# A seventh seven-product unit in the second half of the FFNs' second product

## The chip, the cores and the metric

The kernel runs on one core of a Trainium2 chip. The metric is the device time of one execution in microseconds. Every run is timed alone; the number shown is the median of several runs.

## The reference

One decoder layer on a sequence of 256 tokens with a model width of 2048, in float32: a gated FFN half-step, a mixer of two linear-attention branches, and a second gated FFN half-step. Each of them has a norm on its input and a norm on its output before the residual add. The change touches the FFNs alone:

```
def swiglu(x, w_gate, w_up, w_down):
    return (jax.nn.silu(x @ w_gate) * (x @ w_up)) @ w_down

f1 = swiglu(rms_norm(h, ffn1_pre_norm), ffn1_w_gate, ffn1_w_up, ffn1_w_down)
h = h + 0.5 * rms_norm(f1, ffn1_post_norm)
```

The hidden width is 5504. So the second product of an FFN, the one with w_down, is 256 x 5504 by 5504 x 2048.

## The kernel before

**Products in three parts.** Each float32 operand is split in two: hi, a copy rounded to the type that TensorE multiplies (ScalarE, L153), and lo, the rest (VectorE, L155). A product of two operands is then three matmuls: hi by hi, lo by hi, and hi by lo (L159, L160, L161). One matmul takes a 128 x 128 piece of the activations and 512 columns of weights.

**Units and sevens.** The 256 tokens are two blocks of rows (t = 0, 1). The contraction is cut into k-tiles of 128; two of them are a unit. For one unit and 1024 columns of weights (two blocks of 512) the plain way has eight products: two k-tiles, two blocks of rows, two blocks of columns. The other way is that of Strassen and Winograd: seven products of sums of blocks, and some additions. Here it is the method `seven` of the class `Blocks`. It loads four blocks of weights (four loads of 256 KB on SP's queue), makes the sums of weights on VectorE (all of them through `add`, L245, so the trace shows them under that line: `wsum`, `raw`, `wsum`), splits them on ScalarE (L280 to L286) and VectorE (`wlo`, `wsuml`), and issues 21 matmuls. Four of the seven products gather in accumulators of their own (`p1`, `p5`, `p6`, `p7`), which `share` and `close` add to the four outputs at the end. A plain unit loads its weights in two pieces of 512 KB and issues 24 matmuls.

A seven needs four sums of the activations too (`four_sums`: d, s2, s3, s4, L205 to L208), split into hi and lo. They depend on the unit alone and not on the columns of the weights.

**The second product.** `down_proj` runs over the output in two halves of 1024 columns (`hf`). Each half goes through the 43 k-tiles in order. A list of units says which go by seven products; before a unit on the list is reached, `sums_of` makes its sums, unless they are kept from the first half. Before the change the first half had the units 3, 7, 9, 11, 15 and 19, the second 3, 5, 7, 11, 13 and 15. The sums of 3, 7, 11 and 15 were kept for both halves: three sets in tiles that had held the FFN's input (`xhi0`, `xlo0`, `xhi1`, half of each used) and the fourth in two of the three `tmp` tiles. The sums of the other units lay in the ring of four tiles (`hkhi`, `hklo`) that also takes the split activations of each unit.

The last seven k-tiles of the second half (36 to 42, `DTAIL`) have their weights split ahead into tiles that have become free (`held`), so that the products of the first block of rows can end before those of the second begin, and its norm can start. The first of these tiles is in `xhi1`. The weights pass through rings of five tiles each: `raw` (as loaded), `whi`, `wlo`. The sums of weights of a seven lie in three `row` tiles, of which there are three.

**What sets the order.** Each engine works through its own list of instructions in order. The list is set at build time by a planner, which may move an instruction ahead of others that wait; the program gives the dependences and a rank. At the end of the second half of the first FFN the loads and splits of the mixer's first weights (`following`, `w_in`) are issued between the last products.

Of the kernel before, what the change touches and what calls it, by code (L numbers as in the profile page):

```python
# [7 lines left out]
F32 = mybir.dt.float32  # L8
F32R = mybir.dt.float32r
# [7 lines left out]
P = 128  # L17
# [7 lines left out]
CB = 512  # L25
# [7 lines left out]
AHEAD = 3  # L33
SUMS = (2, 4, 6)
FOUR = (2, 4, 5, 6)
DSUMS = (3, 7, 11, 15)
DMORE = ((9, 19), (5, 13))
DTAIL = 7
O_GQ, O_GK, O_GV, O_GO, O_CODE = 0, 512, 1024, 2048, 3072
O_HQ, O_HF, O_HI, O_HO, O_ZG, O_ZH = 3088, 4112, 5136, 6160, 7184, 9232  # L40
# [48 lines left out]
def kernel(ctx: ExitStack, tc: tile.TileContext, a: dict, out: bass.AP):  # L89
# [9 lines left out]
    work = ctx.enter_context(tc.tile_pool(name="work", bufs=2))  # L99
# [5 lines left out]
    def nm(s):  # L105
        uid[0] += 1
        return f"{s}_{uid[0]}"
# [102 lines left out]
    def operand_sums(x, new_part, out, more=True):  # L210

        yield
        for units in [SUMS] + [(u,) for u in FOUR if more and u not in SUMS]:
            if units[0] in out:
                continue
            n = len(units)
            us = slice(units[0], units[-1] + 1, units[1] - units[0] if n > 1 else 1)
            ab = row_tile("sums").rearrange("p i c -> p (i c)")[:, :4 * n * P].rearrange(  # L220
                "p (t u k) -> p t u k", t=NT, u=n)
            for t in range(NT):
                hi, lo = [part[t].bitcast(F32).rearrange("p (u i) c -> p u (i c)", i=2)[:, us, :]
                          for part in x[:2]]
                nc.vector.tensor_tensor(ab[:, t], hi, lo, op=ALU.add)
                yield
            s = row_tile("sums").rearrange("p i c -> p (i c)")[:, :4 * n * P].rearrange(
                "p (m u c) -> p m u c", m=4, u=n)
            four_sums(*[ab[:, t, :, i * P:(i + 1) * P] for t in range(NT) for i in range(2)],
                      *[s[:, m] for m in range(4)])  # L230
            for j, u in enumerate(units):
                yield
                hi, lo = new_part(0), new_part(1)
                split_into(hi, lo, s[:, :, j, :])
                out[u] = hi, lo
# [145 lines left out]
    def row_tile(s, dt=F32):  # L381
        return rows.tile([P, 3, CB], dt, tag="row", name=nm(s))
# [20 lines left out]
    def tiles4(x):  # L403
        return x.rearrange("p (k c) -> p k c", c=P)
# [12 lines left out]
    def joined(dst, turned):  # L417

        nc.scalar.activation(dst.bitcast(U16).rearrange("p j (k h) -> p h j k", h=2),
                             turned.rearrange("p (h j) k -> p h j k", h=2), AF.Copy)  # L420
# [11 lines left out]
    def lhs_of(x):  # L432
        def lhs(t, kt):

            side.until(lambda: x[2][t] > kt)
            return x[0][t][:, kt, :], x[1][t][:, kt, :]
        return lhs
# [167 lines left out]
    def down_proj(w_dram, nkt, lhs, sums_of, post, pre, wpost, ys, homes, following):  # L605
# [30 lines left out]
        for hf in range(2):  # L636
# [4 lines left out]
            n = nkt - DTAIL if hf else nkt  # L641
            units = sorted(DSUMS + DMORE[hf])
            kt = 0
# [49 lines left out]
    def ffn(pre, x, rs, post, pre_next, begin=None, ready=(), then=None):  # L693
        with ExitStack() as fctx:
            fwork = fctx.enter_context(tc.tile_pool(name=nm("fwork"), bufs=2, reuse_waits="tile"))
            fpool = fctx.enter_context(tc.tile_pool(name=nm("fpool"), bufs=1, reuse_waits="tile"))
            sums = {}

            def new_part(i):
                s = ("hkhi", "hklo")[i]  # L700
                return fwork.tile([P, 2, NT * P], F32R, tag=s, name=nm(s), bufs=4)

            def x_sums():
                return operand_sums(
                    x, lambda i: tiles4(new_part(i).rearrange("p i c -> p (i c)")), sums)

            raws = begin(x_sums) if begin else ()

            def held(w):
                hi, lo = [fpool.tile([P, 2, w], F32R, tag="hT", name=nm("held"), bufs=11)  # L710
                          for _ in range(2)]
                return [(hi, lo)]

            xl = lhs_of(x)
            hT = {}

            blocks = [FIRST] + list(range(0, FIRST, CB))

            def finish(t, f0, w, u, s):
                n = w // P  # L720
                nc.vector.scalar_tensor_tensor(s[:, :w], u[:, :w], rs[t], s[:, :w],
                                               op0=ALU.mult, op1=ALU.mult)
                yield
                turned = turn(s[:, :w], fwork.tile([P, CB], F32, tag="halves", name=nm("halves")))
                for _ in range(6):
                    yield
                joined(hT[f0 // CB][:, :n, t * P:(t + 1) * P], turned)

            for j, f0 in enumerate(blocks):
                w = min(CB, DFF - f0)  # L730
                following = [first_of(a[pre + s], f1) for f1 in blocks[j + 1:j + 2]
                             for s in ("_w_gate", "_w_up")]
                if j or begin:
                    g, u, ready = gemm_pair(
                        [(a[pre + "_w_gate"], f0), (a[pre + "_w_up"], f0)], w, xl, sums, ready,
                        following, () if j else raws, (FOUR if j % 2 else SUMS) if j else ())
                else:
                    g = gemm_block(a[pre + "_w_gate"], f0, w, xl, held=held, ready=ready)
                    ready = ()
                s = []  # L740
                for t in range(NT):
                    st = fwork.tile([P, CB], F32, tag="silu", name=nm("silu"))
                    nc.scalar.activation(st[:, :w], g[t][:, :w], AF.Silu, scale=rs[t])
                    s.append(st)
                if not (j or begin):
                    side.spawn(x_sums())
                    u = gemm_block(a[pre + "_w_up"], f0, w, xl)
                hT[f0 // CB] = fpool.tile([P, 4, NT * P], F32, tag="hT", name=nm("hT"), bufs=11)
                for t in range(NT):
                    side.spawn(finish(t, f0, w, u[t], s[t]))  # L750
            def lhs():
                parts = {}

                def get(t, kt):
                    g2 = kt // 2
                    if g2 not in parts:
                        n = min(2, FKT - g2 * 2)
                        hi, lo = new_part(0), new_part(1)
                        c = g2 % 2 * 2
                        split_into(hi[:, :n, :], lo[:, :n, :], hT[g2 // 2][:, c:c + n, :])  # L760
                        parts[g2] = hi, lo
                    hi, lo = parts[g2]
                    return hi[:, kt % 2, t * P:(t + 1) * P], lo[:, kt % 2, t * P:(t + 1) * P]
                return get


            def in_x(s, dt):
                return tpool.tile([P, 4, CB], dt, tag=s, name=nm("held"))

            wpost = in_x("xlo1", F32)  # L770
            def sums_of(u):
                v = hT[u // 2][:, u % 2 * 2:u % 2 * 2 + 2, :]
                f = row_tile("sums")[:, 0, :]
                four_sums(v[:, 0, :P], v[:, 1, :P], v[:, 0, P:], v[:, 1, P:],
                          *[f[:, k * P:(k + 1) * P] for k in range(4)])
                if any(u in more for more in DMORE):
                    hi, lo = [new_part(i).rearrange("p i c -> p (i c)") for i in range(2)]
                elif u != DSUMS[-1]:
                    home = in_x(("xhi0", "xlo0", "xhi1")[DSUMS.index(u)], F32R)
                    hi, lo = home[:, 0, :], home[:, 1, :]  # L780
                else:
                    hi, lo = [work.tile([P, CB], F32R, tag="tmp", name=nm("sums"), bufs=3)
                              for _ in range(2)]
                split_into(hi, lo, f)
                return tiles4(hi), tiles4(lo)

            def held_x(w):
                v = in_x("xhi1", F32R)
                return [(v[:, 0:2, :], v[:, 2:4, :])]

            ytags = ["halves", "halves", "silu", "silu"]

            def ys():
                return fwork.tile([P, CB], F32, tag=ytags.pop(), name=nm("y"))

            return down_proj(a[pre + "_w_down"], FKT, lhs, sums_of, post, pre_next,
                             [wpost[:, n, :] for n in range(4)], ys,
                             [held_x] + [ring_alloc] * 2 + [held] * 4, then)
# [588 lines left out]
```

## Time and profile before

| | us |
|---|---|
| median of 3 runs | 2067.72 (2065.52 to 2069.54) |
| the profiled execution, its own time | 2064.64 |
| its span, first to last instruction | 2062.7 |
| TensorE busy (matmuls) | 2046.9 |
| VectorE busy | 1857.5 |
| ScalarE busy | 1321.9 |
| first FFN, second product | about 455 to 678 |
| last FFN, second product | about 1816 to 2054 |

The page gives each engine's busy time as a union of its instructions, in which matmuls overlap each other; it says where TensorE waits and not how fast it works. In a group of instructions the first number behind the bar is the busy time, then the mean length of one in ns, and behind the second bar the idle time of the engine just before these instructions and what ended it. In a row of the timeline the first two numbers are the start and the length in us. In a row of stretches each engine has its busy time with the count of its instructions in brackets.

### The profile page before, as it was taken

How to read it: one execution, taken by the hardware profiler on the slowest of the kernel's cores; microseconds unless marked ns; L12 is line 12 of the kernel's file. 1: busy time of each engine (PE TensorE's matmuls, PEld its weight loads, DVE VectorE, ACT ScalarE, POOL GpSimd, SP SyncE). 2: the span in 40 equal slices, each digit the busy share in tenths (PEclk: the TensorE clock that was granted, in tenths of full speed). 3: DMA queues.
4: the chain of work that ended last, by engine and by line, in shares of the span. 5: the costliest groups of instructions: out<-in, count | busy, mean ns of one | idle time of the engine just before them, and what ended most of it. 6: DMA issues, size and time to landing. Idle time of an engine off the chain costs nothing. (4 is left out here: it accounts for less than half of the span.)

```text
span 2062.7 us, 28952 instructions
## 1 busy us (share of the span) xinstructions
PE 2046.9 (99%) x10305; PEld 1700.0 (82%) x10305; DVE 1857.5 (90%) x2187; ACT 1321.9 (64%) x1730; POOL 41.1 (2%) x87
## 2 busy tenths in 40 slices
PE   9999999999999999999999999999999999999998
PEld 9888888888888888878888887788888888888886
DVE  7999999998999789989999896678999999989996
ACT  7666666666666576577655556665666666766663
POOL 1000000000000100000000000010000000000000
PEclk9999999999999999999999999999999999999999
DMA  8767677776767467556565668846767767776663
GB/s 261 217 207 240 194 222 219 210 229 208 232 194 233 143 200 225 155 181 187 173 202 183 186 220 212 258 158 202 230 195 217 228 210 220 222 239 191 212 210 129
DMA packets 254553, 425.60 MB, mean 206 GB/s; under 512 B 71924, under 2 KB 80311, under 8 KB 254408
## 3 DMA queue, kind: packets, MB, share of 16 engines
q1 hardware_dynamic: 194896, 401.80, 61.7%
q10 hardware_dynamic: 59512, 21.94, 5.4%
q8 instruction: 81, 1.33, 0.3%
q14 instruction: 64, 0.52, 0.1%
HBM read 406.11 MB, written 4.19 MB: 199 GB/s over the span
## 5 line engine op out<-in xcount | busy, mean ns | idle before, releaser
L155 DVE TENSOR_TENSOR wlo<-raw,whi 128x1024 fp32r<-128x1024 f32 (+3 forms) x498 | 582.9, 1185 | 69.0 <-ACT whi L153 66.9
L153 ACT ACTIVATE whi<-raw 128x1024 fp32r<-128x1024 f32 (+3 forms) x498 | 504.2, 1025 | 193.7 <-PE c L160 67.1
L159 PE MATMUL c<-whi,xhi 128*128 128x512 f32 (+1 forms) x1270 | 494.6, 390 | 0.0
L160 PE MATMUL c<-whi,xlo 128*128 128x512 f32 (+1 forms) x1270 | 491.3, 387 | 0.0
L161 PE MATMUL c<-wlo,xhi 128*128 128x512 f32 (+1 forms) x1270 | 491.3, 387 | 0.0
L245 DVE TENSOR_TENSOR wlo<-raw,whi 128x1024 fp32r<-128x1024 f32 x252 | 299.6, 1219 | 35.2 <-ACT whi L284 22.3
L161 PEld LDWEIGHTS c<-wlo,xhi 128*128 128x128 f32 x1270 | 238.4, 188 | 47.5
L159 PEld LDWEIGHTS c<-whi,xhi 128*128 128x128 f32 x1270 | 238.4, 188 | 47.0 <-ACT xhi L487 0.6
L160 PEld LDWEIGHTS c<-whi,xlo 128*128 128x128 f32 x1270 | 238.5, 188 | 46.3
L284 ACT ACTIVATE whi<-raw 128x1024 fp32r<-128x1024 f32 x126 | 133.1, 1056 | 199.7 <-DVE raw L245 98.3
L245 DVE TENSOR_TENSOR wsuml<-wsum,wsumh 128x1536 fp32r<-128x1536 f32 x126 | 220.8, 1752 | 8.4 <-ACT wsumh L286 8.4
L161 PE MATMUL c<-wlo,hkhi 128*128 128x512 f32 x558 | 217.2, 389 | 0.0
L159 PE MATMUL c<-whi,hkhi 128*128 128x512 f32 x558 | 217.2, 389 | 0.0
L160 PE MATMUL c<-whi,hklo 128*128 128x512 f32 x558 | 217.1, 389 | 0.0
L282 ACT ACTIVATE wsumh<-wsum 128x1024 fp32r<-128x1024 f32 x126 | 132.6, 1052 | 89.6 <-DVE wsum L245 65.7
L280 ACT ACTIVATE whi<-raw 128x1024 fp32r<-128x1024 f32 x126 | 132.4, 1051 | 62.7 <-PE c L160 49.6
L245 DVE TENSOR_TENSOR wsum<-raw,raw 128x1024 f32<-128x1024 f32 x126 | 153.7, 1219 | 15.7 <-DMA raw<-in_ffn_w_down_dram 13.8
L159 PEld LDWEIGHTS c<-whi,hkhi 128*128 128x128 f32 x558 | 104.8, 188 | 21.8
L161 PEld LDWEIGHTS c<-wlo,hkhi 128*128 128x128 f32 x558 | 104.8, 188 | 21.8 <-DVE wlo L245 0.3
L160 PEld LDWEIGHTS c<-whi,hklo 128*128 128x128 f32 x558 | 104.8, 188 | 21.7
L245 DVE TENSOR_TENSOR c<-c,psum 128x512 f32<-128x512 f32 x135 | 87.4, 693 | 10.4 <-PE c L161 10.1
L245 DVE TENSOR_TENSOR wsum<-raw 128x512 f32<-128x512 f32 x126 | 87.0, 691 | 3.6
(346 smaller groups left out, 3166.3 us busy)
## 6 DMA issues: line engine op xcount, KB each, us to landing
raw<-in_ffn_w_down_dram SPq DMA_DIRECT2D x124, 512.0 KB, 4.7
raw<-in_w_in_dram SPq DMA_DIRECT2D x104, 512.0 KB, 4.5
raw<-in_ffn_w_gate_dram SPq DMA_DIRECT2D x90, 512.0 KB, 4.7
raw<-in_ffn_w_up_dram SPq DMA_DIRECT2D x90, 512.0 KB, 4.3
raw<-in_ffn_w_gate_dram SPq DMA_DIRECT2D x140, 256.0 KB, 3.9
raw<-in_ffn_w_up_dram SPq DMA_DIRECT2D x140, 256.0 KB, 3.6
raw<-in_w_in_dram SPq DMA_DIRECT2D x128, 256.0 KB, 3.6
raw<-in_ffn_w_down_dram SPq DMA_DIRECT2D x96, 256.0 KB, 3.8
```

The costliest lines, as they stand in the source:

```text
L153: last[0] = nc.scalar.activation(hi, src, AF.Copy)
L155: nc.vector.tensor_tensor(lo, src, hi.bitcast(F32), op=ALU.subtract)
L159: nc.tensor.matmul(ps, lhsT=xhi, rhs=whi, start=start, stop=False)
L160: nc.tensor.matmul(ps, lhsT=xlo, rhs=whi, start=False, stop=False)
L161: nc.tensor.matmul(ps, lhsT=xhi, rhs=wlo, start=False, stop=stop)
L245: return nc.vector.tensor_tensor(o, x, y, op=op)
L280: nc.scalar.activation(ahi, ra, AF.Copy)
L282: nc.scalar.activation(hi[:, 0:2, :], wsum[:, 0:2, :], AF.Copy)
L284: nc.scalar.activation(bhi, rb, AF.Copy)
```

## The change

Unit 9 joins the units whose sums are kept, so the list of the second half becomes 3, 5, 7, 9, 11, 13, 15; that of the first half stays as it is. In the second half the k-tiles 18 and 19 thus go through `seven` in place of `plain`. The five kept sets of sums lie in pairs in the three input tiles: 3 and 7 in `xhi0`, 9 and 11 in `xlo0`, 15 in `xhi1`. No set lies in a `tmp` tile any more, and that of unit 9 no longer takes a place in the ring.

```
-DSUMS = (3, 7, 11, 15)
-DMORE = ((9, 19), (5, 13))
+DSUMS = (3, 7, 9, 11, 15)
+DMORE = ((19,), (5, 13))
...
-            wpost = in_x("xlo1", F32)
+            wpost, homes = in_x("xlo1", F32), []
...
-                if any(u in more for more in DMORE):
+                if u in DSUMS:
+                    i = DSUMS.index(u)
+                    if i % 2 == 0:
+                        homes.append(in_x(("xhi0", "xlo0", "xhi1")[i // 2], F32R))
+                    hi, lo = [homes[-1][:, 2 * (i % 2) + k, :] for k in range(2)]
+                else:
                     hi, lo = [new_part(i).rearrange("p i c -> p (i c)") for i in range(2)]
-                elif u != DSUMS[-1]:
-                    home = in_x(("xhi0", "xlo0", "xhi1")[DSUMS.index(u)], F32R)
-                    hi, lo = home[:, 0, :], home[:, 1, :]
-                else:
-                    hi, lo = [work.tile([P, CB], F32R, tag="tmp", name=nm("sums"), bufs=3)
-                              for _ in range(2)]
                 split_into(hi, lo, f)
```

## The prediction

> **What bounds the kernel now.** I read the page first, then busy time by stretches (the first half of the second product in the first FFN, the mixer, four stretches of that FFN's second half: units 3 to 6, 7 to 10, 11 to 15, and what follows), then what TensorE waited for.
>
> ```profile
> span 2062.7 us, 28952 instructions
> PE 2046.9 (99%) x10305; PEld 1700.0 (82%) x10305; DVE 1857.5 (90%) x2187; ACT 1321.9 (64%) x1730; POOL 41.1 (2%) x87
> ...
> PEclk9999999999999999999999999999999999999999
> ```
> ```profile
> core 0: us, PE busy (x) PEld busy (x) DVE busy (x) ACT busy (x) POOL busy (x), PEclk, DMA share, GB/s
> 455.00:567.00 112.00, 112.00 (x494) 92.26 (x493) 100.71 (x127) 71.48 (x88) 0.00 (x0) 1.00 0.71 221
> 678.00:1500.00 822.00, 816.58 (x4836) 677.59 (x4835) 716.12 (x940) 518.29 (x773) 28.77 (x57) 1.00 0.64 195
> ...
> 585.60:606.00 20.40, 20.40 (x92) 16.90 (x91) 19.58 (x23) 14.62 (x19) 0.00 (x0) 1.00 0.56 176
> 606.00:627.00 21.00, 21.00 (x95) 17.38 (x94) 18.85 (x24) 12.17 (x14) 0.00 (x0) 1.00 0.74 234
> 627.00:652.20 25.20, 25.20 (x113) 20.88 (x112) 24.11 (x25) 18.23 (x23) 0.00 (x0) 1.00 0.68 212
> 652.20:678.00 25.80, 25.01 (x110) 20.22 (x109) 19.32 (x23) 11.37 (x16) 1.20 (x4) 1.00 0.71 239
> ```
> ```profile
> PE acc L159 <- ACT whi L153: 2.7, 1, 2.7
> ...
> PE c L160 <- DVE hklo L155: 0.8, 1, 0.8
> PE p L161 <- DVE wsuml L245: 0.6, 1, 0.6
> ```
>
> TensorE never pauses in the sevens of these halves, at a full granted clock. It starts a matmul every 112.00 / 494 = 0.227 us; a row's 0.39 us is the length of one matmul in a pipe, not its price. But VectorE is close behind: 24.11 of 25.20 us (96%) while units 11 to 15 run. And the second half of the first FFN ends with a wait of TensorE (0.8 us as idle time, 1.1 by starts, below) on VectorE's hklo.
>
> **The change, part by part.** In both FFNs, k-unit 9 (two k-tiles) of the second half goes from plain to seven products. The sums of its left operand were made in the first half already, so no sums are added there.
>
> *TensorE.* A plain unit is 2 k-tiles x 4 products x 3 = 24 matmuls, a seven 7 x 3 = 21. Three go per FFN: 3 x 0.227 = 0.68 us, 1.36 us in all. They go out of an engine without pauses, so this is the most that TensorE alone can give.
>
> The Trainium skill, page "TensorE: Matmul & The Clock Gate", section "Wait — 56ns, not 53.3ns?", gives N / 2.4 GHz + 2.5 ns between starts, 215.7 ns at 512 columns. An estimate by that page would be 6 x 0.2157 = 1.29 us; the trace's 0.227 decides.
>
> *VectorE and ScalarE.* The two splits of weights (whi on ScalarE, wlo on VectorE) stay. What a seven has beyond a plain unit:
>
> ```profile
> L245 DVE TENSOR_TENSOR wsuml<-wsum,wsumh 128x1536 fp32r<-128x1536 f32 x126 | 220.8, 1752 | 8.4 <-ACT wsumh L286 8.4
> L245 DVE TENSOR_TENSOR wsum<-raw,raw 128x1024 f32<-128x1024 f32 x126 | 153.7, 1219 | 15.7 <-DMA raw<-in_ffn_w_down_dram 13.8 <-DMA raw<-in_w_in_dram 1.2 <-DMA raw<-in_ffn_w_up_dram 0.4
> L282 ACT ACTIVATE wsumh<-wsum 128x1024 fp32r<-128x1024 f32 x126 | 132.6, 1052 | 89.6 <-DVE wsum L245 65.7 <-PE c L160 18.5 <-DVE raw L245 3.9
> L245 DVE TENSOR_TENSOR wsum<-raw 128x512 f32<-128x512 f32 x126 | 87.0, 691 | 3.6
> L245 DVE TENSOR_TENSOR raw<-wsum,raw 128x512 f32<-128x512 f32 x126 | 86.8, 689 | 2.8
> L286 ACT ACTIVATE wsumh<-wsum 128x512 fp32r<-128x512 f32 x126 | 77.7, 617 | 5.5 <-DVE wsum L245 5.5
> ```
>
> VectorE: 1.752 + 1.219 + 0.691 + 0.689 = 4.35 us. Its instructions overlap by 0.08 us (below: wsuml from 644.65 for 1.75, the next from 646.32), so four of them take 4.03 us of its time. ScalarE: 1.052 + 0.617 = 1.67 us, hidden, for it is idle 7 us in 25.
>
> *Is there room on VectorE?* The lead is the time from the end of wsuml to the first matmul that reads it. Rows of VectorE and TensorE: first half of the first FFN, unit 11; its second half, units 7 and 15.
>
> ```profile
> 515.50 1.75 DVE L245 TENSOR_TENSOR wsuml<-wsum,wsumh 128x1536 fp32r<-128x1536 f32 x1
> ...
> 516.92 0.39 PE L160 MATMUL p<-wsumh,held 128*128 128x512 f32 x1
> 517.31 0.50 PE L161 MATMUL p<-wsuml,held 128*128 128x512 f32 x1
> 517.64 0.39 PE L159 MATMUL p<-wsumh,held 128*128 128x512 f32 x1
> ...
> 604.30 1.75 DVE L245 TENSOR_TENSOR wsuml<-wsum,wsumh 128x1536 fp32r<-128x1536 f32 x1
> 609.25 0.39 PE L161 MATMUL p<-wsuml,held 128*128 128x512 f32 x1
> ...
> 644.65 1.75 DVE L245 TENSOR_TENSOR wsuml<-wsum,wsumh 128x1536 fp32r<-128x1536 f32 x1
> 646.32 0.69 DVE L155 TENSOR_TENSOR hklo<-hT,hkhi 128x512 fp32r<-128x512 f32 x1
> 650.72 0.39 PE L161 MATMUL p<-wsuml,sums 128*128 128x512 f32 x1
> ```
>
> At unit 7 the lead is 609.25 - 606.05 = 3.2 us, at unit 15 it is 650.72 - 646.40 = 4.3. The added seven takes 4.03 of it, and TensorE comes 0.68 earlier. What can give it back is idle time of VectorE:
>
> ```profile
> 615.62 1.23 DVE L245 TENSOR_TENSOR wsum<-raw,raw 128x1024 f32<-128x1024 f32 x1 [2.08 <-DMA raw<-in_ffn_w_down_dram]
> 649.11 1.23 DVE L155 TENSOR_TENSOR held<-raw,held 128x1024 fp32r<-128x1024 f32 x1 [0.97 <-ACT held L153]
> 657.90 0.69 DVE L155 TENSOR_TENSOR hklo<-hT,hkhi 128x512 fp32r<-128x512 f32 x1 [1.13 <-ACT hkhi L153]
> ```
>
> So at unit 15 it is 4.3 - 0.68 - 4.03 = -0.4 us with nothing regained, +1.7 with the 2.08 us. I take a value between, with no stall at the sevens. Where a lead is gone, the price is small: at 517 us it was 0.06 us, and the starts came 0.39 and 0.33 us apart in place of 0.227, 0.27 us lost.
>
> *What is late next: the end of the half.* After unit 15 come four plain k-tiles (48 matmuls, 10.9 us), then seven k-tiles whose weights are split ahead into held tiles. In the first FFN that end is VectorE's already:
>
> ```profile
> 665.93 1.06 ACT L153 ACTIVATE whi<-raw 128x1024 fp32r<-128x1024 f32 x1 [1.17 <-DMA raw<-in_w_in_dram]
> 666.89 0.40 ACT L153 ACTIVATE hkhi<-hT 128x256 fp32r<-128x256 f32 x1
> ...
> 667.35 0.51 PE L159 MATMUL c<-held,hkhi 128*128 128x512 f32 x1
> 668.16 0.42 DVE L155 TENSOR_TENSOR hklo<-hT,hkhi 128x256 fp32r<-128x256 f32 x1
> 668.64 0.50 PE L160 MATMUL c<-held,hklo 128*128 128x512 f32 x1 [0.79 <-DVE hklo L155]
> ...
> 2035.88 0.43 DVE L155 TENSOR_TENSOR hklo<-hT,hkhi 128x256 fp32r<-128x256 f32 x1 [0.68 <-ACT hkhi L153]
> 2039.54 0.39 PE L160 MATMUL c<-held,hklo 128*128 128x512 f32 x1
> ```
>
> The last activation split (k-tile 42) stands on ScalarE behind a mixer weight that waits for its load, and TensorE stands from 667.35 to 668.64: 1.29 - 0.23 = 1.06 us. That load was issued when VectorE freed its slot. Whatever VectorE is later there, this point is later, and the 0.68 us of the first FFN are not seen. Bounds for the first FFN's end: -1.8 us (0.68 gained, and the wait of 1.06 gone because the two queues come out in another order), +4.0 (nothing regained). With the 2.08 us regained it is +1.95; with the 0.97 and 1.13 too (4.18 idle in all, against 4.03 added), 0. I take 0: the nearest row is the stretch of units 3 to 6, where a seven and a plain unit take turns as they now will up to 15, and VectorE is busy 19.58 of 20.40 us there, more than in the 18.85 of 21.00 behind it. The last FFN has a lead of 2039.54 - 2036.31 = 3.2 us at the same place and no loads behind it: -0.68, or 4.03 - 3.23 = +0.8 with nothing regained.
>
> *Loads.* Two of 512 KB become four of 256 KB.
>
> ```profile
> raw<-in_ffn_w_down_dram SPq DMA_DIRECT2D x124, 512.0 KB, 4.7
> ...
> raw<-in_ffn_w_down_dram SPq DMA_DIRECT2D x96, 256.0 KB, 3.8
> ```
>
> Both kinds stand on SP's queue. The DMA share is 0.74 at unit 9 and 0.56 where sevens and plain units take turns, so they cost nothing while the lead lasts; a late one costs as much as the 2.08 us above. The Trainium skill, page "DMA: Bandwidth & Descriptors", section "Bandwidth", asks for transfers of 1 MiB or more, which speaks against the change. The trace agrees in kind, 3.8 us for half of what takes 4.7. By that rule nothing would be regained, which is the slower rival below.
>
> *Homes of the sums.* Sets 3, 7, 9, 11, 15 lie in pairs in xhi0, xlo0, xhi1; set 9 leaves the ring of hkhi/hklo, set 15 the tmp tiles. No row has a wait on these tmp tiles, so 0 for that. The price is in xhi1: its next user, the held tile of k-tile 36 (VectorE 649.11), now waits for unit 15's product p7 (about 651) instead of unit 11's; TensorE reads it after the 48 matmuls, so there are some 10 us of cover, and VectorE has other work then. Between 0 and 2 us of VectorE's time; 0 taken. The three row tiles that a seven fills (wsum, wsumh, wsuml) come free when TensorE has done the unit before, so wsumh of unit 11 now waits for unit 9 (the 18.5 us behind PE c in the row above are such waits). Behind it on ScalarE stand the next weights; from 3 to 7 that cost TensorE nothing, 0 taken.
>
> **Sum.** First FFN 0, last FFN -0.68: -0.7 us. The profiled execution took 2064.64 us (span 2062.7 and 1.9 around it), 3.1 below the median of the runs, 2067.72; by it 2063.9, by the median 2067.0.
>
> **The rivals.**
> 1. *All of TensorE's gain is seen*, and perhaps the wait of 1.06 us goes: -1.4 to -2.4, 2066.3 to 2065.3 us. For it: no pause in any seven of these halves. Against it: VectorE's 96%.
> 2. *The end of the first FFN slides* with only the 2.08 us regained: +1.95 - 0.68 = +1.3, 2069.0. For it: the loads there go out as VectorE frees their slots, a rigid chain.
> 3. *Slower: VectorE becomes the bound* from unit 9 to k-tile 42 in both FFNs, nothing regained: +4.0 and +0.8 = +4.8, 2072.5. It decides once less than about 0.7 us of the 4.03 is taken up by idle time. Against it: 4.18 us are idle.
> 4. *The mixer's order shifts.* The instructions of an engine are ordered at build time, so an edit in the first FFN may re-sort what follows. The mixer's idle TensorE time is 822.00 - 816.58 = 5.4 us; half of it lost or won is 2.7. With rival 1 and all of that it could be 2062.
>
> That the seventh unit isn't taken is excluded: the list of units of the second half then holds 9, and its set is there.
>
> **How the numbers follow.** Within 0.2% (4.1 us) a measurement of this kernel can't be told from no change. Forecast (-0.7, give or take 0.7) 0.40, rival 1 0.25, rival 2 0.18, rival 3 0.11, rival 4 beyond these 0.06. Faster by over 0.2% needs rival 1 and most of the mixer's 5.4 us: 0.07. Slower by over 0.2% is rival 3 and a tail of rivals 2 and 4: 0.13. Same: 0.80. The range goes from 2063.0 (rival 1's far end with the runs' scatter of 2) to 2071.5 (most of rival 3 left out).
>
> **What would show it.** Right: six fewer matmuls; 8 more VectorE instructions, two of each of the four kinds; leads at units 9 to 15 between 0 and 3 us without waits on wsuml of more than 0.3 us; the 2.08 us before a wsum gone; TensorE's wait on the last hklo of the first FFN nearer 2 us than 1. Wrong: the wait gone (rival 1), over 3 us (2), over 4 or a new wait on wsuml of 1 us (3); a mixer longer or shorter by over 1 us (4).

## The result and the profile after

The changed kernel's median is 2063.83 us (20 runs, 2060.12 to 2067.03); that of the kernel before, over 20 runs, is 2067.51. The ratio is 0.9984, with a 95% interval of 0.9978 to 0.9991, which is 3.3 us less (1.9 to 4.5). A second timing, below, gave the same ratio (1.4 to 5.2 us less). The kernel's profiled execution took 2067.03 us, the longest of the 20, and the one of before 2064.64, below the median: the two spans (2065.2 and 2062.7) can't be subtracted, only their stretches.

The page of the kernel after, its first lines:

```profile
span 2065.2 us, 28965 instructions
...
PE 2046.2 (99%) x10299; PEld 1697.1 (82%) x10299; DVE 1864.5 (90%) x2195; ACT 1324.6 (64%) x1734; POOL 41.0 (2%) x87
```

Six matmuls fewer, eight instructions of VectorE and four of ScalarE more: the change does what it says. The stretches of the first FFN's second half (units 3 to 6, 7 to 10, 11 to 15, the rest), in the columns of the prediction:

```profile
core 0: us, PE busy (x) PEld busy (x) DVE busy (x) ACT busy (x) POOL busy (x), PEclk, DMA share, GB/s
586.90:607.30 20.40, 20.40 (x91) 16.89 (x90) 19.58 (x23) 14.63 (x19) 0.00 (x0) 1.00 0.55 174
607.30:627.70 20.40, 20.40 (x91) 16.89 (x90) 20.37 (x23) 12.02 (x14) 0.00 (x0) 1.00 0.75 232
627.70:652.90 25.20, 25.20 (x113) 20.84 (x112) 24.47 (x29) 18.30 (x24) 0.00 (x0) 1.00 0.64 190
652.90:677.40 24.50, 24.50 (x110) 20.24 (x109) 21.18 (x24) 12.77 (x17) 1.20 (x4) 1.00 0.81 282
```

TensorE has no pause, while VectorE is busy 64.42 of the first 66.0 us; before it was 62.54 of 66.6. So VectorE's idle time there went from 4.06 to 1.58 us: 1.9 us of the added work went into it, and 0.6 us is the shorter stretch. The other half of the added work came later: the fourth stretch has 21.18 us of VectorE, where it had 19.32 before. The lead at unit 15 in the timeline of after:

```profile
647.03 1.76 DVE L245 TENSOR_TENSOR wsuml<-wsum,wsumh 128x1536 fp32r<-128x1536 f32 x1
...
651.31 0.39 PE L161 MATMUL p<-wsuml,held 128*128 128x512 f32 x1
```

It is 651.31 - 648.79 = 2.5 us, 1.8 less than before. The leads at 9, 11, 13 and 15 are 3.6, 4.6, 2.7 and 2.5 us, to 0.03 us the same in both FFNs and in a third profile.

The leads at 9 and 11 are above the 0 to 3 us that the prediction named.

Three stretches carry the change. **A** is the first FFN from unit 3's first matmul in the second half to the first transpose of the norm behind it (in before 585.67 to 678.07, in after 586.93 to 677.38). **B** is the last FFN from unit 3's first matmul to the last matmul (1957.71 to 2054.04, 1960.27 to 2055.92). **The close** is from the start of the last matmul to the end of the span. Each row is one profile:

| | A | B | close | span |
|---|---|---|---|---|
| before | 92.40 | 96.33 | 8.70 | 2062.7 |
| before, second profile | 91.29 | 96.33 | 8.70 | 2062.3 |
| after | 90.44 | 95.65 | 9.32 | 2065.2 |
| after, second profile | 90.45 | 95.65 | 9.33 | 2063.3 |
| after, third profile | 90.45 | 95.65 | 9.32 | 2062.9 |
| sums' places only | 91.13 | 96.33 | 8.68 | 2061.3 |
| seventh unit only | 90.45 | 95.65 | 9.34 | 2060.5 |
| before, other order at the end | 91.13 | 96.33 | 8.69 | 2063.4 |
| after, old order at the end | 92.19 | 95.65 | 9.30 | 2063.1 |
| after, four loads split in two | 90.45 | 95.65 | 8.72 | 2064.9 |

### The profile page after: what moved, and what is told of

It is laid out like the page before. It is cut to its first block, busy times and chain, and to the rows that moved or that the text cites. A ratio compares the mean times of both kernels' runs of the same rounds, so it can differ in the third digit from the quotient of the medians.

```text
span 2065.2 us, 28965 instructions
## 1 busy us (share of the span) xinstructions
PE 2046.2 (99%) x10299; PEld 1697.1 (82%) x10299; DVE 1864.5 (90%) x2195; ACT 1324.6 (64%) x1734; POOL 41.0 (2%) x87
## 5 line engine op out<-in xcount | busy, mean ns | idle before, releaser
L245 DVE TENSOR_TENSOR wlo<-raw,whi 128x1024 fp32r<-128x1024 f32 x256 | 304.0, 1219 | 36.0 <-ACT whi L284 22.8
L284 ACT ACTIVATE whi<-raw 128x1024 fp32r<-128x1024 f32 x128 | 135.2, 1056 | 219.2 <-DVE raw L245 115.0
L161 PE MATMUL c<-wlo,hkhi 128*128 128x512 f32 x542 | 211.0, 389 | 0.0
L159 PE MATMUL c<-whi,hkhi 128*128 128x512 f32 x542 | 211.0, 389 | 0.0
L160 PE MATMUL c<-whi,hklo 128*128 128x512 f32 x542 | 210.9, 389 | 0.0
L280 ACT ACTIVATE whi<-raw 128x1024 fp32r<-128x1024 f32 x128 | 134.6, 1051 | 60.0 <-PE c L160 43.4
```

The source lines that it names most:

```text
L159: nc.tensor.matmul(ps, lhsT=xhi, rhs=whi, start=start, stop=False)
L160: nc.tensor.matmul(ps, lhsT=xlo, rhs=whi, start=False, stop=False)
L161: nc.tensor.matmul(ps, lhsT=xhi, rhs=wlo, start=False, stop=stop)
L245: return nc.vector.tensor_tensor(o, x, y, op=op)
L280: nc.scalar.activation(ahi, ra, AF.Copy)
L284: nc.scalar.activation(bhi, rb, AF.Copy)
```

## The experiments

**The places of the sums alone (homes_only), and the seventh unit alone (seven_only).** The first takes the new sets and keeps the old lists of units; the second adds unit 9 and puts only its set in a free half tile.

```
homes_only (edit to the kernel after):
+DLIST = ((3, 7, 9, 11, 15, 19), (3, 5, 7, 11, 13, 15))
...
-units = sorted(DSUMS + DMORE[hf])
+units = DLIST[hf]

seven_only (edit to the kernel before; home3[0] is the tile of set 3, half used):
-DMORE = ((9, 19), (5, 13))
+DMORE = ((9, 19), (5, 9, 13))
...
+if u == 9:
+    hi, lo = home3[0][:, 2, :], home3[0][:, 3, :]
```

> The five sets of sums lie in pairs as in the changed kernel, but the second half keeps the units 3, 5, 7, 11, 13, 15: only where sums lie is changed. Stretch A is the second half of the first FFN, from the first matmul of unit 3 to the first transpose of the norm behind it (92.40 us before, 90.45 after the change). Stretch B is that of the last FFN, from the first matmul of unit 3 to the last matmul (96.33 and 95.65). Theory 1 (the seventh unit, and an order of ScalarE's list that follows from it, make the gain): A 92.4 with TensorE's wait of about 1.1 us on the last hklo still there, B 96.3, time within 1 us of before. Rival (the freed tmp tiles and ring places make the gain): A near 91.3 without the wait, time 1 to 3 us below.

> Unit 9 of the second half by seven products, with the sums' places as before: set 9 in the unused half of set 3's tile, set 11 in its own, set 15 in tmp tiles. Theory 1: all of the change: A 90.4 to 90.6, B 95.6, ratio as that of the change, 0.998 to 0.999. Rival (the places of the sums matter): A 91.7, that is the 0.68 us of three matmuls alone, with the wait of 1.1 us still there.

homes_only: 2063.64 us, ratio 0.9989 (0.9980 to 0.9998). B is 96.33 as before, but A is 91.13: the wait on the last hklo isn't there. Its timeline:

```profile
667.36 0.43 DVE L156 TENSOR_TENSOR hklo<-hT,hkhi 128x256 fp32r<-128x256 f32 x1 [1.23 <-ACT hkhi L154]
...
668.24 0.39 PE L161 MATMUL c<-held,hklo 128*128 128x512 f32 x1
```

(Its line numbers are one higher.) ScalarE's order is still two weights of the mixer ahead of hkhi; hklo is there at 667.79, 0.45 us ahead of its matmul. seven_only: 2063.30 us, 0.9986 (0.9977 to 0.9995); its three stretches are those of the kernel after to 0.02 us. So the seventh unit gives A = 90.45 and B = 95.65, and the places of the sums give nothing to B; but the wait of 1.06 us went in a kernel without it too. Of homes_only, A near 91.3 and a time 1 to 3 us below before's are what the rival expected. By time alone homes_only, seven_only and the kernel after can't be told apart: their intervals overlap, so no time here says which part of the change made the 3.3 us.

**The order at the end of the half, put the other way in both kernels (before_order, after_back).**

```
before_order (edit to the kernel before, at both places of following):
+split_last = last[0]
...
+with tc.issue_after(split_last.ins):
     ready.append(following(len(ready)))

after_back (edit to the kernel after):
+if following is not None and kt == nkt - 1:
+    early = [following(j) for j in range(2)]
+    with tc.issue_after(last[0].ins):
+        lhs_h(0, kt)
```

> The kernel before, with one edge more for the order of ScalarE: the splits of the mixer's first weights come behind the split of k-tile 42's activations. Nothing of the work is changed. Theory 1: the wait of TensorE on the last hklo goes, A 91.2 to 91.4 (1.06 to 1.2 us less), B 96.3 as before, time about 1.1 us less. Rival (VectorE is late there by itself, whatever stands ahead on ScalarE): the wait keeps at least half, A over 91.8.

> The changed kernel with ScalarE's order at that place put back: two splits of the mixer's weights ahead of k-tile 42's. Theory 1: a wait of TensorE on the last hklo of 1 to 2.5 us comes back, A 91.5 to 93, B 95.65 as with the change. If VectorE is late by the added 4 us there (rival 2 of the prediction), the wait is 3 us or more and A over 93.3. If the order doesn't matter, A stays at 90.45.

before_order: 2066.18 us, 0.9999 (0.9990 to 1.0008), A 91.13. after_back: 2066.14 us, 0.9996 (0.9987 to 1.0005), A 92.19, where the timeline has the wait:

```profile
667.88 0.74 PE L159 MATMUL c<-held,hkhi 128*128 128x512 f32 x2 [1.02 <-ACT hkhi L153]
```

So this order can cost the 1.75 us by which after_back's A is longer than the kernel after's. That it is what the kernel before pays doesn't follow: the time of before_order is not shown to differ from before's (the 1.1 us of the theory lie within its interval).

**Each kernel once more (before_again, after_again, after_third).** Nothing is edited.

> The kernel before, unchanged, profiled a second time. Theory (the wait on the last hklo belongs to that kernel's order of instructions, since the load of the mixer's weights ahead of it lands too late): the two starts are again 0.8 to 1.3 us apart, the first FFN's stretch from unit 3 to the norm is 92.0 to 92.5 us, that of the last FFN 96.33, the close 8.7. Rival (the wait was an accident of one execution, and the change is worth 0.68 us there): 91.1 us without the wait.

> The kernel after, unchanged, profiled a second time. If the stretches that differ between the kernels where the order of instructions is the same (the start 55.81, the mixer 608.01 and the out-projection with its norm 107.67 us, against 55.37, 606.95 and 105.79 before) vary by execution, they come out otherwise here, by 0.5 us or more in one of them, while the first FFN's stretch from unit 3 is again 90.4, the last FFN's 95.65 and the close 9.3, each within 0.2 us. If the change made them, they are again 55.8, 608.0 and 107.7.

> The kernel after, unchanged, timed once more against the kernel before. Theory (what the stretches of both profiles of each kernel show in common: -0.68 us in the last FFN, about -0.85 in the first without the wait on the last hklo and up to -1.95 where an execution of the kernel before has it, +0.62 in the close, so -0.9 to -2.0 us): a ratio of 0.9990 to 0.9996. Rival (the first comparison's 0.9984 holds, with a part that no stretch of the profiles shows): 0.9979 to 0.9988.

The second profile of before has A = 91.29 us. Its timeline at the end of the half:

```profile
665.08 1.06 ACT L153 ACTIVATE whi<-raw 128x1024 fp32r<-128x1024 f32 x1 [0.73 <-DMA raw<-in_w_in_dram]
666.04 0.40 ACT L153 ACTIVATE hkhi<-hT 128x256 fp32r<-128x256 f32 x1
...
667.32 0.41 DVE L155 TENSOR_TENSOR hklo<-hT,hkhi 128x256 fp32r<-128x256 f32 x1
...
667.78 0.50 PE L160 MATMUL c<-held,hklo 128*128 128x512 f32 x1
668.12 0.40 PE L161 MATMUL c<-held,hkhi 128*128 128x512 f32 x1
```

The order is the same (mixer weight, hkhi, hklo, matmul), but the matmul starts 0.05 us behind the end of hklo, and the next start comes 0.34 us later in place of 0.227 (0.1 us lost). The rival is right: the wait of 1.06 us belonged to one execution, and hangs on when a load lands. In the kernel after hklo has 0.47 us to spare:

```profile
665.92 0.40 ACT L153 ACTIVATE hkhi<-hT 128x256 fp32r<-128x256 f32 x1
...
666.43 1.06 ACT L153 ACTIVATE whi<-raw 128x1024 fp32r<-128x1024 f32 x1
667.19 0.42 DVE L155 TENSOR_TENSOR hklo<-hT,hkhi 128x256 fp32r<-128x256 f32 x1
...
668.08 0.39 PE L160 MATMUL c<-held,hklo 128*128 128x512 f32 x1
```

The order is another one here: the last split of activations (hkhi, 665.92) now comes ahead of the mixer's first weight (whi, 666.43), so it no longer waits for that weight's load. It is so in seven_only too, while homes_only has before's order: the seventh unit brings this order with it.

A, B and the close of after repeat to 0.01 us. Elsewhere the stretches vary. Where the order of instructions is that of before: the start (up to the first matmul with a sum of weights) took 55.81, 54.96 and 54.80 us in the three profiles of after, 55.37 and 54.78 in the two of before; the mixer (up to the last matmul with its output oT) 608.01, 608.31 and 606.99, against 606.95 and 607.24. The out-projection with its norm (from there to the norm's last transpose) took 107.67, 107.89 and 107.91, against 105.79 and 106.40, but 107.90 in before_order and 105.51 in seven_only: it doesn't go with the change, and it is longer in the kernel that is faster. The first half of the first FFN's second product (from unit 3's first matmul to that of unit 3 in the second half) has the same units in both kernels and varies too, with short waits of TensorE on VectorE's wlo and wsuml: 113.32 and 114.15 us in before, 113.88, 113.24 and 112.95 in after, up to 115.59 in after_four. In the last FFN it took 112.88 to 112.94 in these six. after_third timed 2064.36 us, ratio 0.9984 (0.9975 to 0.9993): the rival's value, that of the first comparison, came again, and the theory's -0.9 to -2.0 us are less than the measured -3.3, though the interval reaches into the theory's range.

**The close (after_four).** In the lists of instructions, a DMA reports on one of eight semaphores in turn, and SP waits for each of them at the end. The kernel after has four more DMAs on SP's queue, so the last stores report on others. This kernel issues four of the mixer's loads in two pieces each: eight more than before.

```
+loads[0] += 1
-for i in range(2) if apart else [slice(0, 2)]:
+for i in range(2) if apart or 300 <= loads[0] < 304 else [slice(0, 2)]:
```

> The kernel after with four of the mixer's loads of 512 KB issued as two of 256 KB each, so that the number of DMAs on SP's queue ahead of the last stores goes up by four and the semaphores on which the last stores report take turns as they did in the kernel before. Theory (the stretch from the last matmul to the end of the span is 9.32 us in the kernel after in place of 8.70 because SP's closing waits stand in another order against the landings): 8.7 us, 0.6 less, stretches in the FFNs as in the kernel after (90.4 and 95.65 within 0.2). Rival (the 0.62 us vary by execution): 9.3 or between, without order.

The ends of before, after and after_four in their timelines (span 2062.7, 2065.2 and 2064.9 us):

```profile
2054.04 0.39 PE L161 MATMUL c<-held,hkhi 128*128 128x512 f32 x1
...
2058.96 0.74 DVE L528 SCALAR_TENSOR_TENSOR h<-y,r,h 128x512 f32<-128x512 f32 x1
```
```profile
2055.92 0.39 PE L161 MATMUL c<-held,hkhi 128*128 128x512 f32 x1
...
2060.83 0.74 DVE L528 SCALAR_TENSOR_TENSOR h<-y,r,h 128x512 f32<-128x512 f32 x1
```
```profile
2056.13 0.39 PE L163 MATMUL c<-held,hkhi 128*128 128x512 f32 x1
...
2061.05 0.74 DVE L530 SCALAR_TENSOR_TENSOR h<-y,r,h 128x512 f32<-128x512 f32 x1
```

From the start of the last matmul to that of VectorE's last instruction it is 4.92, 4.91 and 4.92 us in all three; from that one's end to the end of the span 3.04, 3.67 and 3.07. So the 0.62 us lie behind the last computation, and four DMAs more give 0.60 of them back, as the theory has it. Over the profiles the close is 8.7 to 8.8 with as many DMAs as before or eight more, 9.3 to 9.4 with four more; one kernel with four more (load7_kept, below) had 8.98, which the theory doesn't explain. The time, 2063.49 us (0.9989; 0.9981 to 0.9998), can't be told from the kernel after's.

**How much more VectorE can take (load7, load7_kept).** load7 puts seven additions that nothing reads behind the last split ahead of unit 9. load7_kept also keeps the sums of unit 13, which replaces 19 in the first half.

```
load7 (edit to the kernel after):
+if hf and u == 9:
+    s0, s1 = [work.tile([P, CB], F32, tag="tmp", name=nm("load"), bufs=3) for _ in range(2)]
+    nc.gpsimd.memset(s0, 0.0)
+    with tc.issue_after(last_lo[0].ins):
+        for _ in range(7):
+            nc.vector.tensor_tensor(s1, s0, s0, op=ALU.add)

load7_kept (edit to load7):
-DSUMS = (3, 7, 9, 11, 15)
-DMORE = ((19,), (5, 13))
+DSUMS = (3, 7, 9, 11, 13, 15)
+DMORE = ((), (5,))
```

> The kernel after with seven more additions of 128x512 on VectorE, on tiles that nothing reads, behind the last split of weights ahead of unit 9 in the second half of both FFNs (work added, none left out). Seven at 0.69 us less 0.08 of overlap are 4.27 us, about what one more seven takes of VectorE. Theory (VectorE had regained by idle time all that it could; what is left at unit 15 is the measured lead of 2.5 us): the lead there is gone, waits on wsuml or hklo of 1 to 3 us appear, the first FFN's stretch (unit 3 to the norm) goes from 90.4 to 91.5 to 93.5 us and the last FFN's from 95.65 to 96 to 97.5; 2 to 5 us slower than the kernel after. Rival (VectorE still has idle time to give): both stretches within 0.3 us of the kernel after's, the lead at unit 15 over 0.5 us, no difference in time.

> The kernel with the seven more additions on VectorE ahead of unit 9 (4.27 us, read by nothing), and unit 13's sums kept from the first half, which has 13 in place of 19. With the additions alone the first FFN's stretch was 92.99 and the last FFN's 98.21 us, with a wait of 2.4 us on hkhi of unit 12 behind the making of unit 13's sums. Theory (that chain, sums on VectorE, their split on ScalarE, the split of unit 12 behind it, is what is late, and VectorE as a whole still has time): without the sums of 13 the wait is gone, 90.4 to 90.9 and 95.6 to 96.1 us. Rival (VectorE as a whole has no time left): another wait of 0.5 to 2 us takes its place, 91 to 92.5 and 96.2 to 97.7 us.

load7: 2070.93 us, 1.0025 (1.0016 to 1.0034); A 92.99, B 98.21, 2.55 longer each. That is 7.4 us more than after_four, timed beside it, and more than the theory's 2 to 5. The lead at unit 15 isn't what went (it is 1.9 us here). TensorE stands once in each FFN, at plain unit 12. The timeline of load7 (line numbers one higher):

```profile
632.52 0.28 DVE L209 TENSOR_TENSOR sums<-hT,sums 128x128 f32<-128x128 f32 x1
...
632.84 0.63 ACT L154 ACTIVATE hkhi<-sums 128x512 fp32r<-128x512 f32 x1 [3.31 <-DVE sums L209]
633.38 1.14 ACT L154 ACTIVATE hkhi<-hT 128x512 fp32r<-128x512 f32 x2
...
634.04 0.73 PE L160 MATMUL c<-whi,hkhi 128*128 128x512 f32 x2 [2.03 <-ACT hkhi L154]
```

and the same place in the kernel after:

```profile
629.47 0.63 ACT L153 ACTIVATE hkhi<-sums 128x512 fp32r<-128x512 f32 x1 [0.65 <-DVE sums L208]
630.01 1.14 ACT L153 ACTIVATE hkhi<-hT 128x512 fp32r<-128x512 f32 x2
...
632.49 0.39 PE L159 MATMUL c<-whi,hkhi 128*128 128x512 f32 x1
```

The split of unit 12's activations (hkhi<-hT) stands on ScalarE behind the split of unit 13's sums, and that one waits for VectorE. In after the first of the two (0.61 us) ends at 630.62 and is read at 632.49: 1.87 us to spare, the same to 0.02 us in both FFNs and in all kernels with the seventh unit. In before it was 6.5 and 8.1. So the tightest place isn't the lead on wsuml (2.5) but this one, and 4.27 - 1.87 = 2.4 us is about what load7 lost there in each FFN.

load7_kept: 2069.15 us, 1.0022 (1.0012 to 1.0031). The wait on hkhi is gone. A is 91.46 and B 96.10: of the 2.55 us 1.0 and 0.45 are left, in the first FFN most of it at the end of the half:

```profile
669.59 0.50 PE L161 MATMUL c<-held,hklo 128*128 128x512 f32 x1 [0.50 <-DVE hklo L156]
```

So the chain was the first to be late, as the theory has it, and with it gone VectorE as a whole is late by 0.5 to 1 us, which is the rival's. The time hardly shows it, since unit 13 costs 1.6 and 1.4 us in the first half (from unit 11 to unit 3, the stretch measured for fourteen below, it takes 73.09 and 72.83 us in place of 71.49 and 71.40).

**More such units (eight, fourteen).** eight adds unit 1 to the second half (its sums made there); fourteen adds 13 to the first half and keeps its sums.

```
eight (edit to the kernel after):
-DMORE = ((19,), (5, 13))
+DMORE = ((19,), (1, 5, 13))

fourteen (edit to the kernel after):
-DSUMS = (3, 7, 9, 11, 15)
-DMORE = ((19,), (5, 13))
+DSUMS = (3, 7, 9, 11, 13, 15)
+DMORE = ((19,), (5,))
```

> The kernel after with unit 1 too by seven products in the second half, its sums made there (four more additions of sums, two splits of them, and four additions of weights on VectorE, about 5 us in all), at a place where VectorE's lead comes from the end of the first half. Stretches from the first matmul of unit 19 in the first half: 119.69 us to the first transpose of the norm in the first FFN, 124.89 to the last matmul in the last FFN, in the kernel after. Theory (a seven is worth three matmuls, 0.68 us, wherever VectorE is ahead, and it is): 119.0 and 124.2 us, 1.4 us less in all. Rival (the lead at the start of the half is used up by the sums): waits at units 1 to 5, both stretches 0.3 to 2 us longer than the kernel after's.

> The kernel after with a sixth kept set: the sums of unit 13 are made in the first half, kept in the free half of the third input tile, and unit 13 goes by seven products in the first half too, so both halves have seven such units (3, 7, 9, 11, 13, 15, 19 and 3, 5, 7, 9, 11, 13, 15). Stretch from unit 11's first matmul with a sum of weights in the first half to unit 3's in the second: 71.49 us (518.16 to 589.65) and 71.39 (1891.59 to 1962.98) in the kernel after. Theory (three matmuls, 0.68 us, wherever no chain is late; eight more DMAs than in the kernel before bring the close back to 8.7): 70.8 and 70.7 us, the second half as in the kernel after (90.45 and 95.65), the close 8.7; 2.0 us less than the kernel after. Rival (VectorE's lead in the first half, busy 90% there, is gone behind unit 13 as it was behind unit 1 with eight sevens): waits of 1 to 3 us at units 13 to 19, the stretch 72 to 74 us, 1 to 5 us more than the kernel after.

eight: 2073.16 us, 1.0035 (1.0022 to 1.0048). The stretches from unit 19 are 125.51 and 129.51 us, 5.8 and 4.6 longer: the rival's direction, at more than twice its 2 us. Stretches of eight in the first FFN (a standstill of TensorE, what follows, what follows that) and in the last:

```profile
590.80:594.20 3.40, 0.48 (x3) 0.04 (x1) 3.40 (x8) 1.14 (x3) 0.00 (x0) 1.00 0.82 270
594.20:597.40 3.20, 3.14 (x7) 2.49 (x8) 3.20 (x6) 3.20 (x6) 0.00 (x0) 0.50 0.51 167
597.40:600.60 3.20, 3.20 (x15) 2.66 (x14) 3.20 (x3) 2.28 (x3) 0.00 (x0) 0.96 0.34 65
...
1965.10:1968.50 3.40, 0.41 (x3) 0.01 (x1) 3.40 (x8) 1.21 (x3) 0.00 (x0) 1.00 0.78 266
1968.50:1969.70 1.20, 1.20 (x5) 0.90 (x6) 1.20 (x3) 1.20 (x2) 0.00 (x0) 1.00 0.74 256
1969.70:1973.00 3.30, 3.30 (x9) 2.65 (x9) 3.30 (x5) 3.15 (x6) 0.00 (x0) 0.51 0.17 58
```

TensorE stands 3.4 us between two starts at unit 4, again behind the split of another unit's sums (those of unit 5, made here), and then runs at half its clock for 3.4 us (the second row lies wholly in this phase).

fourteen: 2066.16 us, 1.0006 (0.9997 to 1.0015). The close is 8.75 and A and B are 90.45 and 95.65, as the theory has them, but the first half isn't: from unit 11 to unit 3 it takes 73.90 and 72.41 us in place of 71.49 and 71.39. The rival is right there. VectorE in fourteen, units 11 to 15 of the first half (the first row holds a wait of TensorE of 1.41 us on wlo, at unit 13), and TensorE's wait at unit 15:

```profile
517.00:527.00 10.00, 8.59 (x38) 6.66 (x37) 9.93 (x16) 6.84 (x10) 0.00 (x0) 1.00 0.55 189
527.00:537.00 10.00, 10.00 (x45) 8.00 (x44) 9.87 (x15) 5.44 (x8) 0.00 (x0) 1.00 0.67 211
```
```profile
538.18 0.50 PE L161 MATMUL p<-wlo,hkhi 128*128 128x512 f32 x1 [0.88 <-DVE wlo L245]
```

VectorE is full (99%), and the three matmuls saved are worth less than the wait. None of the kernels tried is shown to be faster than the kernel after.

## Why the prediction was right or wrong

The forecast was -0.7 us, 2067.0; measured were -3.3 (1.9 to 4.5 less), 2063.8. The time lies in the range, 0.8 above its low end, and nearest to rival 1 (-1.4 to -2.4). In the two FFNs it is rival 1 that came: A and B together are 1.5 us shorter than in the second profile of before, 2.6 than in the first, and the sign named for it, no wait on the last hklo, is there. That the whole time lies in the range is in part luck, since 1.3 to 2.4 of its 3.3 us have no known cause (below). Nor was 0.2% beyond telling: twenty runs of each kernel tell 0.16% from no change.

**TensorE, 0.68 us per FFN: right, and seen in both.** B is 0.68 shorter; A is 90.45 against 91.13 in the two kernels without the seventh unit and without the wait.

**The first FFN's end, 0: wrong.** The step that failed is "In the first FFN that end is VectorE's already". It read a wait of 1.06 us in one execution as a property of the kernel. A second profile of the same kernel loses 0.1 us there, and A went from 91.29 to 90.45 (-0.84) in place of 0, or from 92.40 (-1.95) where an execution has the wait. The mechanism (the last split behind a mixer weight that waits for its load) is real: it is in before and after_back. But there it is a matter of when a load lands, and in the kernel after it has no place: the split comes ahead of the mixer's weight. So VectorE's added work didn't make that point later, as the step had it; hklo is there 0.47 us ahead of its matmul.

**VectorE, 4.03 us, with the lead and idle time to take it: right in kind, mis-sized.** No seven waited; the lead at unit 15 is 2.5 us in place of -0.4 to +1.7. The 2.08 us before a wsum are gone, as foretold. But the term "+1.7 with the 2.08 us" took all that wasn't idle time for delay. From unit 3's first matmul to the end of unit 15's wsuml VectorE idled 3.07 us before and 1.59 after, so 1.5 of the 4.03 us went into idle time; about 1.4 came behind that wsuml, since one split of weights (wlo, 1.22 us) has moved there; and wsuml ends 1.1 us later. That and TensorE's 0.68 make the 1.8 us by which the lead is shorter. The Trainium skill, page "DMA: Bandwidth & Descriptors", section "Bandwidth", asks for transfers of 1 MiB or more; that the loads of 256 KB would leave nothing to regain isn't borne out here: no instruction of VectorE waits on a load in the three stretches with sevens. What the prediction left out is the place that had become tightest: it followed wsuml and not the sums that are still made in this half, where 1.87 us are left.

**Homes, 0: right** to 0.2 us (homes_only against the second profile of before: A 91.13 and 91.29, B 96.33 in both).

**The close: not in the sum.** 0.62 us are given back behind the last matmul, nearly all that the last FFN gains.

**Rival 3** (VectorE the bound) was rightly held unlikely for this change, but it is near: load7, with about one seven's worth of VectorE work more, is slower by 2.55 us in each FFN. **Rival 4** isn't shown: the order of instructions differs only in the two second products (and in the turns of the DMAs' semaphores), and the mixer varies as much within one kernel as between the two.

**What stays open.** The stretches give -0.84 - 0.68 + 0.62 = -0.9 us against the second profile of before, -2.0 against the first; measured are -3.3, twice, and of the two sums only -2.0 lies within the intervals (-1.9 to -4.5, -1.4 to -5.2). Of the rest, 1.3 to 2.4 us, no stretch shows a cause. If the wait of 1.06 us, or a longer one, were in most of before's executions, it would be part of it; two profiles can't say. Nor are the profiles typical: the two profiled executions of before took 2064.64 and 2064.20 us, less than its medians (2067.51 and 2065.63 beside them), the three of after 2067.03, 2065.12 and 2064.68, more than its own (2063.83 and 2064.36). Against the wait stands that before_order, whose profile lacks the wait, isn't faster than before. The same sum for the other kernels, against the second profile of before, misses their times too: homes_only -2.3 measured and -0.2 by stretches, load7 +5.2 and +4.3, load7_kept +4.5 and +3.0. So a difference of some 2 us between two kernels is here beyond what the profiles' stretches explain.

## What to carry to other kernels

A short wait in one profile that ends on a load's landing is worth a second profile before a term of the sum is built on it; the stretches that repeat to 0.01 us are those that TensorE paces. When an engine has work added, look for the tightest place along every chain that runs through it, not only along the tiles that the change touches: here it was a split of another unit's sums with an unrelated split queued behind it. And how far the next step can go is measured by dummy work: seven additions showed in one run that VectorE had no room for another unit's work ahead of unit 9, and two kernels with more such units, at other places, were slower than the kernel after.

## What was not expected of the hardware

**A standstill of TensorE can be paid for a second time.** In eight, after 3.4 us between two starts, the granted clock is 0.50 for 3.4 us, and matmuls start 0.427 us apart in place of 0.227. In load7, after 2.42 us between two starts, the next starts are 0.34 us and then 0.227 apart, with no such phase. In the last FFN of eight the slow phase came 1.3 us after the standstill. So a wait of 3.15 us lost about 4.8 us in the first FFN (3.15, and 1.7 in slow starts).

The Trainium skill, page "TensorE: Matmul & The Clock Gate", section "What's actually happening", has the clock halved after an idle window of about 3.4 us, in windows that run free of the kernel. The traces agree with the windows: in every profile the granted clock changes only at whole multiples of 3.41 us from its first change. They don't agree that the window has to be idle: in the last FFN of eight, TensorE was busy for 1.30 us of the window ahead of the slow phase (1966.38 to 1969.79). Nor does the length of the standstill decide. At the end of the mixer TensorE stands in every profile, and a slow phase of 3.4 us or more follows there, or at a second standstill some 17 us behind it, in ten of the fourteen: after 1.65 us between two starts in the second profile of before, but not after 3.12 in the first, nor after 3.19 in the first of after. Over the fourteen profiles, between 60 and 2040 us, the windows ahead of a slow phase held 0.4 to 1.6 us of matmuls, and those without one behind them 1.5 us or more. So it hangs on how the standstill falls into the windows, which differs by execution. The out-projection, in which this slow phase mostly falls, isn't longer for it (105.4 to 108.4 us with it, 105.7 to 107.7 without), so it isn't shown to explain the open rest.

**The number of DMAs moves the end of the span.** Four more on SP's queue cost 0.62 us behind the last instruction of any computing engine, and four more again give 0.60 back; load7_kept, with four more, lost only 0.28.
